# Update of the sample states in a decoder layer: 32-row products against block-masked rows, replaced by 12-row products in four row tiles, with the state index on partitions

## The chip, the cores and the metric

One core of one Trainium2 chip. The metric is the device time of one launch in microseconds (us). The engines of the core are PE (TensorE, matmuls), DVE (VectorE), ACT (ScalarE), POOL (GpSimd) and SP (SyncE). In this kernel SP issues most loads and POOL issues most stores; neither computes anything to speak of.

## The reference

One layer of a hybrid decoder with d_model 2048. 288 token columns go through it: 256 of one prompt and 8 sample sequences of 4 tokens each. Cut to what matters here:

```python
proj = rmsnorm(x) @ w_in                 # s_in, z, xbc, dt, two gates
ya   = sgu_branch(s_in)                  # u * (W_s LN(v) + b)
yb, h_new = mamba_branch(z, xbc, dt, conv_buf, h0)
x = x + (sigmoid(ga) * (ya @ w_out_a) + sigmoid(gb) * (yb @ w_out_b)) @ w_o
x = x + (silu(h2 @ w_gate) * (h2 @ w_up)) @ w_down         # h2 = rmsnorm(x)

# the state of one sample sequence after its four tokens; 64 heads of
# 64 channels p, 128 state numbers n, 8 heads share one group's b_in
h_new[p, n] = exp(cs[last]) * h0[p, n]
            + sum_l  exp(cs[last] - cs[l]) * dt[l] * x[l, p] * b_in[l, n]
```

The change concerns the last line for the sample sequences: 8 sequences x 64 heads x 64 x 128 numbers, 16.8 MB read and as much written. The sum runs over the four tokens of one sequence only. The numbers are fp32 throughout. A product in full precision is made of three quick ones: each operand is split into a high part (rounded to the type fp32r) and a low part, and high x high, high x low and low x high are added.

## The kernel before, in words

**The weight units.** Nearly all of PE's stream is products of weights with 288 token columns: records `pm<-hh,wh` and the like, 128x128 weights against 128x288. The weights come from HBM in pieces of 512 KB (`raw`, four buffers, loaded by SP), ACT casts a piece to `wh`, DVE subtracts to make `wl`, three buffers each. The list `ORDER` sets the sequence of units: input projection (channels u, v, z, x, b, c, gates), the products with w_out_a and w_out_b (`A`, `B`; the rows `yb` are the right sides of w_b), then w_o and the feed-forward part.

**The planner.** Everything else is written as Python generators (`g_ssd`, `g_gate`, `g_upd` and others), and a planner, the class `Plan`, lays them between the weight products when the program is built. It keeps a clock for each engine from rough costs. After each k-step of a unit `side()` asks every open generator, in order of its priority, whether what it waits for (`yield x`: data; `yield "name"`: a milestone) is ready by these clocks, and if so lets it write its next instructions. Before a unit's products `need()` runs the generators until the right side has been written. On the chip every engine then runs its own list strictly in that order, and waits by semaphores where data isn't there. A `yield` in a generator is therefore a place where weight products may be put.

**Buffers.** Tiles come from pools with fixed numbers of buffers: q (25, of 4x288 columns), t (7, of 630 columns), x (4 PSUM banks of 512 columns), m (2 PSUM pairs for the units). `K.res("t")` waits until the planner has one free, `K.rel("t")` and `K.drop()` (for q) give them back. How many a generator asks for thus moves it, and others, in the order.

**Groups.** The state-space part has 8 groups g of 8 heads. `g_ssd(g)` transposes and scales the group's rows; it stores the 32 sample tokens' b rows (`bt`, to `scr_bs`) and their weighted x rows (`xw`, to `scr_xs`) to scratch memory in HBM, and sets the milestone `fin{g}`. `g_gate(g)` makes the gated and normalised rows yb of group g (its norm is the product `rms`), split into `ybh` and `ybl`. `g_upd(g)`, with the lowest priority, starts after the unit marker "late" (behind the gate units `gb`), after `fin{g}` and after `g_upd(g - 1)`.

**The update.** `g_upd(g)` loads `scr_xs` and `scr_bs` three times over into 96 partitions, by six loads on SP's queue: the row blocks 0, 32 and 64 hold high, high and low parts of x against high, low and high parts of b, so that one product of 96 rows has the three terms. `bk` is b laid out eight times, multiplied with a mask (`C_BM`) that keeps the rows of sequence b only. For each pair of heads j of the group there are a load of 512 KB of states `su`, 128 channels on the partitions and 8 sequences x 128 state numbers in the columns, two products `up` of 512 columns, eight instructions `K.stt` that multiply 128x128 of the state with its decay (`etot`, one number for each partition and sequence) and add the product, and a store on POOL's queue. `K.load` uses SP's queue unless told otherwise, `K.store` POOL's.

Of the kernel before, what the change touches and what calls it, by code (L numbers as in the profile page):

```python
# [6 lines left out]
F32 = mybir.dt.float32  # L7
F32R = mybir.dt.float32r
I32 = mybir.dt.int32
AF = mybir.ActivationFunctionType  # L10
ALU = mybir.AluOpType

T, P, S, NB, L = 288, 256, 32, 8, 4
# [2 lines left out]
EPS = 1e-6  # L16


C_ID, C_TRI, C_ONE, C_SUF, C_MB, C_MBS, C_PAR, C_JM, C_BM, C_SEL, C_NEG, C_MP, C_JB = (
    0, 128, 256, 512, 640, 672, 704, 832, 864, 872, 904, 1032, 1160)  # L20
C_W = 1288
V_G1, V_G2, V_GF, V_NG, V_DS, V_CW, V_CB, V_DT, V_AL = 0, 16, 32, 48, 80, 112, 304, 352, 353
V_W = 354

# [383 lines left out]
def trunk(ctx, tc, io):  # L408
    ND = 6
    K = Plan(ctx, tc, io)  # L410
    nc = tc.nc
# [232 lines left out]
    wds = K.const([128, 16], "wds")  # L644
    csm = K.const([128, 8, 2, S], "csm")
    ecs = K.const([128, 64], "ecs")
    etot = K.const([128, 32, NB], "etot")

    def g_dt(ps):
        qa = yield from K.q([4, T], "dta")  # L650
# [70 lines left out]
        for j in range(4):  # L721
            for i in range(2):
# [8 lines left out]
        K.act(et, csr[:, P:T].rearrange("p (b l) -> p b l", l=L)[:, :, 3], AF.Exp)  # L731
        yield et
        K.rel("x", 2)
        em = K.tmp([64, 32, NB], "em")
        K.mul(em, et.unsqueeze(1).to_broadcast([64, 32, NB]),
              cst[0:64, C_JM:C_JM + 32].unsqueeze(2).to_broadcast([64, 32, NB]))
        yield em
        yield from K.res("x")
        pe = K.ps("etot")
        K.mm(pe[:, 0:256], cst[0:64, C_PAR:C_PAR + 128], em.rearrange("p j b -> p (j b)"), True, True)  # L740
        yield pe
        K.copy(etot, pe[:, 0:256].rearrange("p (j b) -> p j b", j=32))
        K.rel("x")
        K.rel("t")
        K.drop(2)
# [108 lines left out]
    def g_ssd(g):  # L854
# [33 lines left out]
        bt = K.tmp([128, 4, 128], "bt")  # L888
        K.copy(bt[:, 0:2], p1[:, 0:P].rearrange("p (c n) -> p c n", c=2))
        K.copy(bt[0:32, 2], p1[0:32, P:384])  # L890
        K.store(io["scr_bs"][g], bt[0:32, 2])
        for c in range(2):
            p1 = K.ps("xt")
            for j in range(4):
# [20 lines left out]
                    K.mm(pf[:, j * 128:j * 128 + 128], xd[:, c, j * 128:j * 128 + 128], bt[:, c], c == 0, c == 1)  # L915
        xw = K.tmp([128, 128], "xw")
        K.mul(pair(xw), pair(xts), wide(wds[:, H2]))
        K.store(io["scr_xs"][g], xw)
        K.sub(ms, csm[:, g], css[:, H2].unsqueeze(2).to_broadcast([128, 2, S]))
        K.ts(ms, ms, 0.0, ALU.min)  # L920
        yield ms
# [101 lines left out]

    def g_upd(g):
        yield ["late", f"fin{g}", f"upd{g - 1}"]
        yield from K.res("q", 2)
        yield from K.res("t", 2)
        xf, b3 = K.tmp([96, 512], "xf"), K.tmp([96, 3, 128], "b3")
        for r in range(3):
            K.load(xf[32 * r:32 * r + 32].rearrange("t (j c) -> t j c", j=4), io["scr_xs"][g].rearrange("(j t) c -> t j c", j=4))  # L1030
            K.load(b3[32 * r:32 * r + 32, 0], io["scr_bs"][g])
        sk = K.q_now([2, 512], f"sk{g}", F32R)[0:96]
        bh = sk[:, 1, 0:128]
        yield [xf, b3]
        K.copy(sk[:, 0], xf)
        K.copy(bh, b3[:, 0])
        yield sk
        K.sub(sk[64:96, 0], xf[64:96], sk[64:96, 0].bitcast(F32))
        K.vcopy(b3[:, 1], bh.bitcast(F32))
        K.sub(b3[32:64, 1], b3[32:64, 0], bh[32:64].bitcast(F32))  # L1040
        sk = sk[:, 0]
        bk = K.q_now([NB, 128], f"bk{g}", F32R)[0:96]
        K.mul(bk, b3[:, 1].unsqueeze(1).to_broadcast([96, NB, 128]),
              cst[0:96, C_BM:C_BM + NB].unsqueeze(2).to_broadcast([96, NB, 128]))
        K.rel("t", 2)
        yield None
        for j in range(4):
            st = yield from K.q([NB, 128], f"su{g}{j}")
            K.load(st, io["st_p"][4 * g + j])
            yield st  # L1050
            yield from K.res("x", 2)
            pu = [K.ps(f"up{i}") for i in range(2)]
            bf = bk.rearrange("p b n -> p (b n)")
            for i in range(2):
                K.mm(pu[i], sk[:, 128 * j:128 * j + 128], bf[:, 512 * i:512 * i + 512], True, True, f32=False)
            yield [st] + pu
            for b in range(NB):
                K.stt(st[:, b], st[:, b], etot[:, 4 * g + j, b:b + 1], pu[b // 4][:, 128 * (b % 4):128 * (b % 4) + 128],
                      ALU.mult, ALU.add)
                if b == 3:  # L1060
                    yield None
            K.rel("x", 2)
            yield st
            K.store(io["new_ssm_s"][4 * g + j], st)
            K.drop()
        K.drop(2)
        K.have.add(f"upd{g}")

    K.have.add("upd-1")
# [303 lines left out]
def _constants():  # L1373
    import numpy as np

    c = np.zeros((128, C_W), np.float32)
    i = np.arange(128)
    c[:, C_ID:C_ID + 128] = np.eye(128)
    c[:, C_TRI:C_TRI + 128] = i[:, None] <= i[None, :]
    c[:, C_ONE:C_ONE + 128] = 1  # L1380
    c[:, C_ONE + 128:C_ONE + 256] = c[:, C_TRI:C_TRI + 128]
    c[:, C_NEG:C_NEG + 128] = np.where(i[:, None] <= i[None, :], 0, -1e30)
    c[:, C_SUF:C_SUF + 128] = i[:, None] > i[None, :]
    s = i[:32]
    blk = s[:, None] // 4 == s[None, :] // 4
    c[:32, C_MB:C_MB + 32] = blk & (s[:, None] <= s[None, :])
    c[:32, C_MBS:C_MBS + 32] = blk & (s[:, None] > s[None, :])

    at = 32 * (s % 16 // 4) + 4 * (s // 16) + s % 4
    c[:32, C_MP + at] = c[:32, C_MB:C_MB + 32]  # L1390
    c[at, C_SEL + s] = 1
    for j in range(4):
        c[32 * j:32 * j + 32, C_JB + 32 * j:C_JB + 32 * j + 32] = blk & (s[:, None] <= s[None, :])
    h = i[:64]
    c[:64, C_PAR:C_PAR + 128] = h[:, None] % 2 == i[None, :] // 64
    c[:64, C_JM:C_JM + 32] = h[:, None] // 2 == s[None, :]
    c[:96, C_BM:C_BM + 8] = (i[:96, None] % 32) // 4 == i[None, :8]
    return c


def _layout(f):
    import numpy as np

    f = {k: np.asarray(v) for k, v in f.items()}
    ca = np.ascontiguousarray
    lay = lambda w: ca(w.reshape(w.shape[0] // 128, 128, w.shape[1] // 256, 256).transpose(2, 1, 0, 3))
    chan = lambda v: v.reshape(-1, 128).T
    x = np.concatenate([f["x_prompt"].reshape(P, D), f["x_sample"].reshape(S, D)], 0)
    w = f["w_in"][0]
    wt = w.reshape(16, 128, w.shape[1])  # L1410
    dev = {}
    dev["x"] = ca(x.T.reshape(16, 128, T).transpose(1, 0, 2))
    vec = np.zeros((128, V_W), np.float32)
    vec[:, V_G1:V_G1 + 16] = chan(f["norm1_g"][0])
    vec[:, V_G2:V_G2 + 16] = chan(f["norm2_g"][0])
    vec[:, V_GF:V_GF + 16] = chan(f["final_norm_g"])
    vec[:, V_NG:V_NG + 32] = chan(f["ssm_norm_g"][0])
    vec[:, V_DS:V_DS + 32] = chan(np.repeat(f["d_skip"][0], 64))
    vec[:, V_CW:V_CW + 192] = f["conv_w"][0].reshape(4, 48, 128).transpose(2, 1, 0).reshape(128, 192)
    vec[:, V_CB:V_CB + 48] = chan(f["conv_b"][0])  # L1420
    vec[64:, V_DT] = f["dt_bias"][0]
    vec[:64, V_AL] = f["a_log"][0]
    dev["vec"] = vec
    dev["cst"] = _constants()
    dev["stc"] = ca(f["state_conv"][0].reshape(24, 48, 128).transpose(2, 1, 0))
    sw = f["sgu_w"][0]
    dev["swt"] = ca(sw.transpose(2, 0, 1))
    swb = np.zeros((128, 16, 32), np.float32)
    for b in range(8):
        swb[4 * b:4 * b + 4, :, 4 * b:4 * b + 4] = sw[:, :4, :4].transpose(2, 0, 1)  # L1430
    dev["swb"] = swb
    dev["sgb"] = ca(f["sgu_b"][0])
    dev["lng"] = ca(f["sgu_ln_g"][0])
    dev["lnb"] = ca(f["sgu_ln_b"][0])
    cols = _win_columns()
    wi = np.empty((len(cols), 128, 16, 256), np.float32)
    for n, c in enumerate(cols):
        wi[n] = wt[:, :, c:c + 256].transpose(1, 0, 2)
    dev["w_in"] = wi
    dev["w_dt"] = ca(wt[:, :, 14336:14400].transpose(1, 0, 2))  # L1440
    dev["w_a"] = lay(f["w_out_a"][0])
    dev["w_b"] = np.stack([lay(f["w_out_b"][0][2048 * i:2048 * i + 2048]) for i in range(2)])
    dev["w_o"] = lay(f["w_o"][0])
    g = f["w_ffn_gate"][0].reshape(16, 128, JT, 128)
    u = f["w_ffn_up"][0].reshape(16, 128, JT, 128)
    dev["w_gu"] = ca(np.stack([g, u], 3).transpose(2, 1, 0, 3, 4).reshape(JT, 128, 16, 256))
    dev["w_d"] = np.stack([lay(f["w_ffn_down"][0][2816 * i:2816 * i + 2816]) for i in range(2)])
    st = f["state_ssm"][0].reshape(8, 8, 512, 128)
    dev["st_n"] = ca(st.transpose(1, 3, 0, 2).reshape(8, 128, 4096))
    dev["st_p"] = ca(f["state_ssm"][0].reshape(8, 32, 128, 128).transpose(1, 2, 0, 3))  # L1450
    return dev


_OUT = {
    "y": (128, 16, T), "new_ssm_p": (8, 128, 512), "new_conv": (128, 48, 27), "new_ssm_s": (32, 128, 8, 128), "new_v": (32, 2048),
}
_SCR = {"scr_cs": (64, T), "scr_a": (8, 128, 2, T), "scr_b": (8, 128, 2, T),
        "scr_xs": (8, 128, 128), "scr_bs": (8, 32, 128),
        "scr_xd": (8, 128, 2, 512), "scr_bt": (8, 128, 2, 128)}


# [30 lines left out]
```

## Time and profile before

| | before |
|---|---|
| median of 3 runs | 2320.87 us (2320.67 to 2321.26) |
| profiled execution, its own time | 2320.45 us |
| its span in the trace | 2318.7 us |
| mean granted TensorE clock | 0.998 |
| PE busy | 2304.2 us, 99% |
| DVE busy | 1431.4 us, 62% |
| ACT busy | 1001.0 us, 43% |
| POOL busy | 88.7 us, 4% |
| HBM read, written | 421.65 MB, 31.54 MB |

How such a profile is read. Times are in us from the start of the span. A group's row has line, engine, operation, output<-inputs by the program's names, sizes, and `x` count; after the first bar the busy time in all and the mean length in ns of one, after the second the idle time of the engine just before them and what ended it. A row of waits has the instruction that waited, `<-` what it waited for, then the sum in us, the count and the longest. A row of the timeline has start and length, engine, line, the instruction; `x16` means that sixteen stand together, and a bracket holds idle time ahead of it. A row of DMA issues has the count, then minimum/median/maximum of the issue in ns, and below the time from issue to landing. A row by windows has the stretch A:B, its length, and for PE, PEld (weight load), DVE, ACT and POOL the busy time with the number of instructions; then the granted clock, the DMA engines' busy share and GB/s. Matmuls are pipelined: one lasts about 0.3 us and the next starts 0.13 us after it.

### The profile page before, as it was taken

How to read it: one execution, taken by the hardware profiler on the slowest of the kernel's cores; microseconds unless marked ns; L12 is line 12 of the kernel's file. 1: busy time of each engine (PE TensorE's matmuls, PEld its weight loads, DVE VectorE, ACT ScalarE, POOL GpSimd, SP SyncE). 2: the span in 40 equal slices, each digit the busy share in tenths (PEclk: the TensorE clock that was granted, in tenths of full speed). 3: DMA queues.
4: the chain of work that ended last, by engine and by line, in shares of the span. 5: the costliest groups of instructions: out<-in, count | busy, mean ns of one | idle time of the engine just before them, and what ended most of it. 6: DMA issues, size and time to landing. Idle time of an engine off the chain costs nothing.

```text
span 2318.7 us, 42525 instructions
## 1 busy us (share of the span) xinstructions
PE 2304.2 (99%) x17571; PEld 2271.5 (98%) x17571; DVE 1431.4 (62%) x2216; ACT 1001.0 (43%) x1425; POOL 88.7 (4%) x187
## 2 busy tenths in 40 slices
PE   9999999999999989999999999999999999999999
PEld 8999999999999989999999999999999999999999
DVE  7687553446887875477865767766664444545444
ACT  6453433335654645455433334433333333333333
POOL 0000000001110000010000000000000000000000
PEclk9999999999999999999999999999999999999999
DMA  8465686666667556565567877676775555555654
GB/s 290 132 210 149 199 285 190 180 185 193 188 188 229 152 168 190 174 189 150 176 216 246 284 239 250 216 222 218 227 227 167 167 170 165 168 165 164 229 168 140
DMA packets 151106, 455.96 MB, mean 197 GB/s; under 512 B 20848, under 2 KB 40560, under 8 KB 150912
## 3 DMA queue, kind: packets, MB, share of 16 engines
q1 hardware_dynamic: 140528, 424.06, 59.5%
q0 software_dynamic: 9376, 27.62, 3.3%
q8 instruction: 137, 2.24, 0.4%
q10 hardware_dynamic: 1008, 1.58, 0.2%
q14 instruction: 57, 0.47, 0.1%
HBM read 421.65 MB, written 31.54 MB: 195 GB/s over the span
## 4 chain that ended last, share of the span: by engine, by line
PE 99%; DVE 1%; DMA 0%; ACT 0%; issue 0%; SPq 0%; ACTq 0%; DVEq 0%
PE pm L187 94%; PE y L187 1%; PE up L187 1%; PE fin L187 1%; PE yoff L187 1%; PE mix L187 0%; PE xt L193 0%; PE cb L187 0%; DMA x<-x 0%; DVE wl L152 0%; PE va L193 0%; PE rms L187 0%; PE btok L193 0%; DVE xs L170 0%; DVE acc L170 0%
## 5 line engine op out<-in xcount | busy, mean ns | idle before, releaser
L152 DVE TENSOR_TENSOR wl<-raw,wh 128x1024 fp32r<-128x1024 f32 (+2 forms) x700 | 835.1, 1193 | 830.3 <-ACT wh L183 822.8
L183 ACT CAST wh<-raw 128x1024 fp32r<-128x1024 f32 (+2 forms) x704 | 717.6, 1020 | 1094.6 <-PE pm L187 796.3
L187 PE MATMUL pm<-hh,wh 128*128 128x288 f32 x2128 | 632.5, 297 | 0.0
L187 PE MATMUL pm<-hl,wh 128*128 128x288 f32 x2128 | 627.6, 295 | 0.0
L187 PE MATMUL pm<-hh,wl 128*128 128x288 f32 x2112 | 623.8, 295 | 0.0
L187 PE MATMUL pm<-xgl,wh 128*128 128x288 f32 x1408 | 415.8, 295 | 0.0
L187 PE MATMUL pm<-xgh,wl 128*128 128x288 f32 x1408 | 415.8, 295 | 0.0
L187 PE MATMUL pm<-xgh,wh 128*128 128x288 f32 x1408 | 414.5, 294 | 0.6 <-DVE ff L152 0.6
L187 PEld LDWEIGHTS pm<-hh,wh 128*128 128x128 f32 x2128 | 400.1, 188 | 9.5 <-issue 8.1
L187 PEld LDWEIGHTS pm<-hl,wh 128*128 128x128 f32 x2128 | 399.7, 188 | 0.2
L187 PEld LDWEIGHTS pm<-hh,wl 128*128 128x128 f32 x2112 | 396.7, 188 | 0.2 <-DVE wl L152 0.2
L187 PEld LDWEIGHTS pm<-xgh,wh 128*128 128x128 f32 x1408 | 264.2, 188 | 1.5 <-issue 0.8
L187 PEld LDWEIGHTS pm<-xgl,wh 128*128 128x128 f32 x1408 | 264.7, 188 | 0.7
L187 PEld LDWEIGHTS pm<-xgh,wl 128*128 128x128 f32 x1408 | 264.4, 188 | 0.0
L187 PE MATMUL pm<-fl,wh 128*128 128x288 f32 x704 | 207.9, 295 | 0.0
L187 PE MATMUL pm<-fh,wl 128*128 128x288 f32 x704 | 207.8, 295 | 0.0
L187 PE MATMUL pm<-fh,wh 128*128 128x288 f32 x704 | 207.2, 294 | 0.0
L187 PE MATMUL pm<-ybh,wh 128*128 128x288 f32 x512 | 153.2, 299 | 6.1 <-ACT ybh L183 6.1
L187 PE MATMUL pm<-ybl,wh 128*128 128x288 f32 x512 | 152.5, 298 | 0.8 <-DVE ybl L152 0.8
L187 PE MATMUL pm<-ybh,wl 128*128 128x288 f32 x512 | 152.4, 298 | 0.0
L187 PEld LDWEIGHTS pm<-fl,wh 128*128 128x128 f32 x704 | 132.3, 188 | 0.0
L187 PEld LDWEIGHTS pm<-fh,wl 128*128 128x128 f32 x704 | 132.2, 188 | 0.0
(254 smaller groups left out, 2809.8 us busy)
## 6 DMA issues: line engine op xcount, KB each, us to landing
raw<-w_in SPq DMA_DIRECT2D x284, 512.0 KB, 4.0
raw<-w_gu SPq DMA_DIRECT2D x176, 512.0 KB, 3.9
raw<-w_d SPq DMA_DIRECT2D x75, 512.0 KB, 3.6
raw<-w_b SPq DMA_DIRECT2D x64, 512.0 KB, 4.4
st<-st_n SPq DMA_DIRECT2D x32, 512.0 KB, 6.3
raw<-w_a SPq DMA_DIRECT2D x32, 512.0 KB, 3.9
su<-st_p SPq DMA_DIRECT2D x32, 512.0 KB, 5.7
new_ssm_s<-su POOLq DMA_DIRECT2D x32, 512.0 KB, 3.4
```

The lines of the kernel that those rows point to most:

```text
L152: self.nc.vector.tensor_tensor(out, a, b, op=op)
L183: self.nc.scalar.copy(out, a)
L187: self.nc.tensor.matmul(out, lhsT, rhs, start=start, stop=stop)
```

## The change

`g_upd` is written anew. The state index n is on the 128 partitions now, and the columns are 8 sequences x 512 channels, the layout that the input `st_n` already has; the input `st_p` goes, and the output `new_ssm_s` changes its layout. A sequence has 4 tokens, so its three terms need 12 rows. Four sequences stand at the partitions 0, 32, 64 and 96, with 12 rows each, and their four products (weights `bk` 12x128, right side `xk` 12x512) go to the array's four row tiles, into four PSUM banks: all of pool x. A group takes two such halves h. The decay `etot` is now the same on all partitions and lies along the columns; DVE multiplies the state with it before the products (two instructions of 1024 columns for a half), and adds the products afterwards (four of 512).

The rows `xk` and `bk` are gathered by 36 loads for each group, on POOL's queue. The splitting in high and low parts moves from `g_upd` to `g_ssd`, which asks for one more t buffer (`xb`) for that, and stores both parts. In `g_dt` the product for `etot` has 512 columns where it had 256.

```diff
@@ g_dt
-        em = K.tmp([64, 32, NB], "em")
-        K.mul(em, et.unsqueeze(1).to_broadcast([64, 32, NB]),
-              cst[0:64, C_JM:C_JM + 32].unsqueeze(2).to_broadcast([64, 32, NB]))
+        em = K.tmp([64, NB, 64], "em")
+        K.mul(em, et.unsqueeze(2).to_broadcast([64, NB, 64]),
+              cst[0:64, C_ID:C_ID + 64].unsqueeze(1).to_broadcast([64, NB, 64]))
...
-        K.mm(pe[:, 0:256], cst[0:64, C_PAR:C_PAR + 128], em.rearrange("p j b -> p (j b)"), True, True)
+        K.mm(pe, K.one[0:64], em.rearrange("p b h -> p (b h)"), True, True)
...
@@ g_ssd
-        K.store(io["scr_bs"][g], bt[0:32, 2])
...
-        K.store(io["scr_xs"][g], xw)
+        yield from K.res("t")
+
+        xb = K.tmp([128, 4, 128], "xb", F32R)
+        K.hilo(xb[0:32, 2], xb[0:32, 3], bt[0:32, 2])
+        K.store(io["scr_bs"][g].rearrange("a t n -> t a n"), xb[0:32, 2:4])
+        yield xw
+        K.hilo(xb[:, 0], xb[:, 1], xw)
+        K.store(io["scr_xs"][g].rearrange("a p c -> p a c"), xb[:, 0:2])
+        K.rel("t")
...
@@ g_upd (the lines before stand above)
+        yield from K.res("q")
+        yield from K.res("t")
+
+        xk, bk = K.q_now([2, 512], f"xk{g}", F32R), K.tmp([128, 2, 128], "bk", F32R)
+        for r in range(4):
+            for i, (a, b) in enumerate(((0, 0), (0, 1), (1, 0))):
+                o = slice(32 * r + 4 * i, 32 * r + 4 * i + 4)
+                for h in range(2):
+                    K.load(xk[o, h].rearrange("l (j c) -> l j c", j=4),
+                           io["scr_xs"][g, a].rearrange("(j h r l) c -> h r l j c", j=4, h=2, r=4)[h, r], nc.gpsimd)
+                K.load(bk[o], io["scr_bs"][g, b].rearrange("(h r l) n -> r l h n", h=2, r=4)[r], nc.gpsimd)
+        yield [xk, bk]
+        for h in range(2):
+            yield from K.res("q", 2)
+            st = [K.q_now([2, 512], f"su{g}{h}{i}") for i in range(2)]
+            for i, t in enumerate(st):
+                K.load(t, io["st_n"][g, :, 2048 * h + 1024 * i:2048 * h + 1024 * i + 1024].rearrange("p (b c) -> p b c", b=2))
+            for i, t in enumerate(st):
+                yield t
+                v = t.rearrange("p b (h d) -> p b h d", h=8)
+                e = etot[:, 4 * h + 2 * i:4 * h + 2 * i + 2, 8 * g:8 * g + 8]
+                K.mul(v, v, e.unsqueeze(3).to_broadcast([128, 2, 8, 64]))
+            yield from K.res("x", 4)
+            pu = [K.ps(f"up{r}") for r in range(4)]
+            for r in range(4):
+                o = slice(32 * r, 32 * r + 12)
+                K.mm(pu[r], bk[o, h], xk[o, h], True, True, f32=False)
+            yield st + pu
+            for i, t in enumerate(st):
+                for k in range(2):
+                    K.add(t[:, k], pu[2 * i + k], t[:, k])
+                K.rel("x", 2)
+                K.store(io["new_ssm_s"][g, :, 2048 * h + 1024 * i:2048 * h + 1024 * i + 1024].rearrange("p (b c) -> p b c", b=2), t)
+                yield None
+            K.drop(2)
+        K.drop()
+        K.rel("t")
         K.have.add(f"upd{g}")
```

What the planner makes of it is not in the diff. The numbers behind names in the following listings count tiles, `DMASW` and `DMAHW` are the semaphores of the DMA lanes (POOL's queue uses eight lanes, DMASW0 to 7, in turn), and a bracket holds what a row waits for.

POOL's queue around the end of one group's update, before: the stores of the states, one for each pair of heads, and each waits for DVE's last instruction on its tile.

```order
L202 DMA new_ssm_s<-su_12988 128x1024 [waits DMAHW3_49,DMASW2_49,DVE_49]
L202 DMA new_ssm_s<-su_13200 128x1024 [waits DMAHW2_49,DMASW3_49,DVE_49]
L202 DMA new_ssm_s<-su_13370 128x1024 [waits DMAHW0_49,DMASW4_49,DVE_49]
L202 DMA new_ssm_s<-su_13646 128x1024 [waits DMAHW7_49,DMASW5_49,DVE_49]
L202 DMA new_ssm_s<-su_13783 128x1024 [waits DMAHW4_49,DMASW6_49,DVE_49]
```

After: the last two stores of a group, and behind them the first of the next group's 36 loads.

```order
L201 DMA new_ssm_s<-su_13037 128x1024 [waits DMAHW5_49,DMASW7_49,DVE_49]
L201 DMA new_ssm_s<-su_13038 128x1024 [waits DMAHW6_49,DMASW0_49,DVE_49]
L196 DMA xk_13230<-scr_xs 4x4x128 [waits DMAHW1_49,DMASW1_49,Activation_49]
L196 DMA xk_13230<-scr_xs 4x4x128 [waits DMASW2_49]
L196 DMA bk<-scr_bs 4x2x128 [waits DMASW3_49]
L196 DMA xk_13230<-scr_xs 4x4x128 [waits DMASW4_49]
L196 DMA xk_13230<-scr_xs 4x4x128 [waits DMASW5_49]
```

The loads stand between the stores of one group and those of the next, and each waits for the landing of the transfer that used its lane before, the eighth ahead of it.

PE's list at one update's products, before (`hh` and `hl` are the high and low parts of the normalised rows):

```order
L187 MATMUL pm<-hh_943,wl 128x288
L187 MATMUL up_13714<-bk_13631,sk_13545 128x512
L187 MATMUL up_13715<-bk_13631,sk_13545 128x512
L187 MATMUL pm<-hh_943,wh 128x288
L187 MATMUL pm<-hl_944,wh 128x288
```

After, at the first half of a group:

```order
L186 MATMUL pm<-hh_943,wl 128x288
L186 MATMUL up_13426<-xk_13230,bk 128x512 [waits DMASW6_49,DMASW4_49,DMASW7_49,DMASW3_49,DMASW1_49]
L186 MATMUL up_13427<-xk_13230,bk 128x512 [waits DMASW5_49,DMASW4_49,DMASW7_49,DMASW2_49,DMASW0_49]
L186 MATMUL up_13428<-xk_13230,bk 128x512 [waits DMASW5_49,DMASW3_49,DMASW6_49,DMASW1_49,DMASW0_49]
L186 MATMUL up_13429<-xk_13230,bk 128x512 [waits DMASW6_49,DMASW4_49,DMASW7_49,DMASW2_49,DMASW1_49]
L186 MATMUL pm<-hh_1051,wh 128x288 [waits Activation_49]
```

Pairs have become fours, and the products wait for the lanes of POOL's loads; the weight products of the unit stand behind them.

PE's list also moved at the first unit of w_b, where the rows of groups 3 and 4 are prepared. Before, ahead of the first of the yb products (62 rows ahead of it) stood the norm's product of gate group 3, then the first products of `g_ssd(4)`:

```order
L187 MATMUL pm<-hh_785,wl 128x288
L187 MATMUL rms<-rmp,oner 128x288 x2
L187 MATMUL cb<-c_3315,bf 128x256
L187 MATMUL cb<-c_3315,bf 128x128
L187 MATMUL cb<-c_3315,sm 128x32
L187 MATMUL pm<-hh_785,wh 128x288
```

After, the same two things stand behind the first 72 yb products:

```order
L186 MATMUL pm<-ybl_8808,wh 128x288
L186 MATMUL pm<-ybh_8617,wl 128x288
L186 MATMUL cb<-c_3315,bf 128x256
L186 MATMUL cb<-c_3315,bf 128x128
L186 MATMUL cb<-c_3315,sm 128x32
L192 MATMUL btok<-cst,bf 128x128 x2
L192 MATMUL btok<-cst,bf 32x128
L192 MATMUL xt<-cst,xs_8802 128x128 x8
L192 MATMUL xts<-cst,sm 128x128
L186 MATMUL rms<-rmp,oner 128x288 x2
L186 MATMUL pm<-ybh_9470,wh 128x288
```

Of the second listing, the products of group 4's preparation (`cb`, `btok`, `xt`, `xts`) and the norm of gate group 3 have come to stand between the yb products of group 2 and those of group 3.

More of the change, by code (lines that the diff above doesn't have):

```diff
@@ L16 @@
 EPS = 1e-6
-C_ID, C_TRI, C_ONE, C_SUF, C_MB, C_MBS, C_PAR, C_JM, C_BM, C_SEL, C_NEG, C_MP, C_JB = (
-    0, 128, 256, 512, 640, 672, 704, 832, 864, 872, 904, 1032, 1160)
-C_W = 1288
+C_ID, C_TRI, C_ONE, C_SUF, C_MB, C_MBS, C_SEL, C_NEG, C_MP, C_JB = 0, 128, 256, 512, 640, 672, 704, 736, 864, 992
+C_W = 1120
 V_G1, V_G2, V_GF, V_NG, V_DS, V_CW, V_CB, V_DT, V_AL = 0, 16, 32, 48, 80, 112, 304, 352, 353
@@ L646, in trunk @@
     ecs = K.const([128, 64], "ecs")
-    etot = K.const([128, 32, NB], "etot")
+    etot = K.const([128, NB, 64], "etot")
     def g_dt(ps):
@@ L739, in g_dt @@
         pe = K.ps("etot")
-        K.mm(pe[:, 0:256], cst[0:64, C_PAR:C_PAR + 128], em.rearrange("p j b -> p (j b)"), True, True)
+        K.mm(pe, K.one[0:64], em.rearrange("p b h -> p (b h)"), True, True)
         yield pe
-        K.copy(etot, pe[:, 0:256].rearrange("p (j b) -> p j b", j=32))
+        K.copy(etot, pe.rearrange("p (b h) -> p b h", b=NB))
         K.rel("x")
@@ L1025, in g_upd @@
         yield ["late", f"fin{g}", f"upd{g - 1}"]
[L1026 to L1065, printed above, removed]
@@ L1066, in g_upd @@
-        K.drop(2)
+        yield from K.res("q")
[8 more added lines that the diff above has]
+                K.load(bk[o], io["scr_bs"][g, b].rearrange("(h r l) n -> r l h n", h=2, r=4)[r], nc.gpsimd)
@@ L1393, in _constants @@
         c[32 * j:32 * j + 32, C_JB + 32 * j:C_JB + 32 * j + 32] = blk & (s[:, None] <= s[None, :])
[L1394 to L1397, printed above, removed]
     return c
@@ L1449, in _layout @@
     dev["st_n"] = ca(st.transpose(1, 3, 0, 2).reshape(8, 128, 4096))
-    dev["st_p"] = ca(f["state_ssm"][0].reshape(8, 32, 128, 128).transpose(1, 2, 0, 3))
     return dev
 _OUT = {
-    "y": (128, 16, T), "new_ssm_p": (8, 128, 512), "new_conv": (128, 48, 27), "new_ssm_s": (32, 128, 8, 128), "new_v": (32, 2048),
+    "y": (128, 16, T), "new_ssm_p": (8, 128, 512), "new_conv": (128, 48, 27), "new_ssm_s": (8, 128, 4096), "new_v": (32, 2048),
 }
 _SCR = {"scr_cs": (64, T), "scr_a": (8, 128, 2, T), "scr_b": (8, 128, 2, T),
-        "scr_xs": (8, 128, 128), "scr_bs": (8, 32, 128),
+        "scr_xs": (8, 2, 128, 128), "scr_bs": (8, 2, 32, 128),
         "scr_xd": (8, 128, 2, 512), "scr_bt": (8, 128, 2, 128)}
@@ L1472 @@
     for n, s in _SCR.items():
-        io[n] = nc.dram_tensor(n, s, F32, kind="Internal").ap()
+        io[n] = nc.dram_tensor(n, s, F32R if n in ("scr_xs", "scr_bs") else F32, kind="Internal").ap()
     with tile.TileContext(nc) as tc, ExitStack() as ctx:
@@ L1479 @@
     sp = o["new_ssm_p"].reshape(8, 128, 4, 128).transpose(0, 2, 1, 3)
-    ss = o["new_ssm_s"].transpose(2, 0, 1, 3)
+    ss = o["new_ssm_s"].reshape(8, 128, NB, 512).transpose(2, 0, 3, 1)
     cv = o["new_conv"].transpose(2, 1, 0).reshape(27, 6144)
```

## The prediction

> **What bounds the kernel now.** I read the page first: engines, clock row, chain.
>
> ```profile
> PE 2304.2 (99%) x17571; PEld 2271.5 (98%) x17571; DVE 1431.4 (62%) x2216; ACT 1001.0 (43%) x1425; POOL 88.7 (4%) x187
> PEclk9999999999999999999999999999999999999999
> PE 99%; DVE 1%; DMA 0%; ACT 0%; issue 0%; SPq 0%; ACTq 0%; DVEq 0%
> ```
>
> TensorE has work from end to end. A change is worth what it takes out of PE's stream, less every microsecond for which PE has to wait. So I next read PE's waits, and the stretch around the longest one by windows.
>
> ```profile
> PE pm L187 <- ACT ybh L183: 6.1, 1, 6.1
> PE pm L187 <- DVE ybl L152: 0.8, 1, 0.8
> ...
> 834.00:841.00 7.00, 7.00 (x55) 7.00 (x54) 5.21 (x14) 3.19 (x4) 1.44 (x3) 1.00 0.53 153
> 841.30:847.40 6.10, 0.00 (x0) 0.00 (x0) 6.00 (x13) 1.61 (x2) 0.67 (x2) 0.76 0.90 283
> 847.40:854.70 7.30, 6.49 (x25) 6.18 (x26) 4.26 (x11) 1.44 (x3) 0.29 (x1) 0.50 0.22 80
> 855.00:862.00 7.00, 7.00 (x55) 7.00 (x54) 4.13 (x6) 6.75 (x16) 0.54 (x1) 1.00 0.41 121
> ```
>
> There is one long wait, 6.1 us, at the first unit of w_b, for the gated rows yb. DVE is busy for 6.00 of it with 13 instructions (0.46 us each). A wait costs more than itself: after it the granted clock is 0.50 for 7.3 us and 25 matmuls pass. At the normal pitch (0.133 us, next fence) they take 3.3, and 0.8 is the second wait, so 3.2 us were lost behind a wait of 6.1.
>
> **The products themselves.** PE's own time for `up`, from the timeline:
>
> ```profile
> 1161.52 0.62 PE L187 MATMUL up<-bk,sk 96*128 96x512 f32 x2
> 1161.97 0.30 PE L187 MATMUL pm<-hh,wh 128*128 128x288 f32 x1
> 1162.11 0.29 PE L187 MATMUL pm<-hl,wh 128*128 128x288 f32 x1
> 1162.23 0.30 PE L187 MATMUL pm<-hh,wl 128*128 128x288 f32 x1
> ```
>
> A pair holds the array from 1161.52 to 1161.97, 0.45 us, 0.225 for each product of 512 columns; 32 pairs are 14.4 us. After the change there are again 64 products of 512 columns, in 16 groups of four. What four cost is open: this trace has no row tiles. The nearest rows are column tiles, the yoff products:
>
> ```profile
> 288.29 0.30 PE L187 MATMUL pm<-hh,wl 128*128 128x288 f32 x1
> 288.51 1.93 PE L187 MATMUL yoff<-st,cm 128*32 128x512 f32 x16
> 290.37 0.40 PE L187 MATMUL pm<-hh,wh 128*128 128x288 f32 x1
> 290.61 0.30 PE L187 MATMUL pm<-hl,wh 128*128 128x288 f32 x1
> ...
> L187 PE MATMUL yoff<-st,cm 128*32 128x512 f32 x128 | 15.4, 598 | 0.0
> ```
>
> 128 records of 598 ns are 76.5 us of work in 15.4 us of busy time: tiles overlap. The switch has a price: 0.22 instead of 0.13 us before the first tile, 0.24 instead of 0.13 behind, and about 0.1 to empty, 0.3 us for both ways. By these rows a group takes 0.225 + 0.3 = 0.53 us, 16 groups 8.4, a gain of 6.0 us. The ends: without any switch price 3.6 us, a gain of 10.8; without overlap 4 x 0.225 + 0.3 = 1.2 us, 19.2 in all, a loss of 4.8. I take the gain of 6.0, by the nearest row.
>
> The Trainium skill's page "TensorE: Matmul & The Clock Gate" (Part 3, measured speedup) gives four row tiles of 512 columns as 3.07 times faster than one after the other. By it a group would take 0.30 us without a switch, and the sum would end 3.5 us lower; no run here shows it.
>
> ```profile
> L187 PE MATMUL etot<-em,cst x2: 376/428/480, 155.9 to 156.2; 64*128 64x256 f32 x2
> ```
>
> The etot product doubles to 512 columns; its two records now stand 0.3 us apart, so +0.6 us, in PE's stream at 156 us.
>
> **What feeds the products.** This is the term that decides. The loads of xk and bk go to POOL's queue, 36 for each g, where six went to SP's. In the program the 36 of group g+1 stand right behind the last store of group g (the listing above). That store waits for DVE's last add of g, and PE's four products of g+1 wait for the loads' lanes; behind them PE has all the weight matmuls queued. So the whole chain from add to products has to fit between two products in PE's stream. Its parts:
>
> ```profile
> L202 POOL DMA_DIRECT2D scr_bs<-bt x8: 511/511/513, 562.3 to 1044.0; - x8
> DMA to landing us min/median/max: 1.7/3.2/4.2
> ...
> L202 POOL DMA_DIRECT2D new_conv<-ncv x48: 537/538/695, 136.0 to 1022.7; - x48
> DMA to landing us min/median/max: 1.7/3.4/5.5
> ...
> 610.22 0.54 POOL L202 DMA_DIRECT2D scr_xd<-xd  x1 [4.35 <-DVE xts L152]
> 610.75 0.54 POOL L202 DMA_DIRECT2D scr_bt<-bt  x1
> ...
> 1062.23 0.54 POOL L202 DMA_DIRECT2D new_ssm_p<-fin  x1 [4.17 <-ACT fin L183]
> ...
> 1162.71 2.15 DVE L170 SCALAR_TENSOR_TENSOR su<-su,etot,up 128x128 f32<-128x128 f32 x8
> 1165.16 0.54 POOL L202 DMA_DIRECT2D new_ssm_s<-su  x1 [102.39 <-DVE su L170]
> ...
> L183 ACT CAST wh<-raw 128x1024 fp32r<-128x1024 f32 x663 | 694.4, 1048 | 1043.5 <-PE pm L187 749.8 <-issue 259.3 <-DMA raw<-w_gu 6.4
> L152 DVE TENSOR_TENSOR wl<-raw,wh 128x1024 fp32r<-128x1024 f32 x663 | 811.2, 1224 | 795.7 <-ACT wh L183 788.3 <-DMA b<-scr_bs 4.0 <-PE pm L187 1.9
> L152 DVE TENSOR_TENSOR xt<-xt,dtk 128x512 f32<-128x512 f32 x16 | 10.9, 683 | 1.2 <-PE xt L193 1.2
> ```
>
> POOL takes 0.51 to 0.54 us for an issue, whatever its size, and two in a row start 0.53 apart. So: 0.3 us from DVE's end (1164.86) to the store (1165.16), 0.5 for the store, 36 x 0.54 = 19.4 for the loads, 3.4 until the last one lands: 23.6 us from the last add.
>
> The room: from the second half's products of g to the first half's of g+1, PE's listing has 157, 145, 157, 211, 163, 193 and 193 matmuls for the seven successions, 174 on average, 23.2 us at 0.133. The adds use up part of it: on DVE they stand behind the next wl, which needs a cast (1.05) and a split (1.22) after PE has freed a buffer, and four adds of at most 0.68 follow; by the matmuls that stand between the products and the adds in the program, the last add ends 5 to 10 us behind the products, 7.1 on average. 16.1 us are left for 23.6. PE waits 7.5 us, seven times: +53 us. The first group pays nothing: POOL's last earlier row is a store at 1062 us.
>
> The bounds of this: issue at 0.51 and landing in 1.7 make 20.9, a wait of 4.8, +34. If landing takes 5.5, it also holds back the issue: each load waits for the lane of the eighth before it, 5.5 / 8 = 0.69 us each, 24.8 + 5.5 + 0.8 = 31.1, a wait of 15, +105.
>
> The page "DMA: Bandwidth & Descriptors" of the Trainium skill (Anatomy of one DMA, SWDGE path) puts about 2.0 us on a small transfer. By it the chain is 22.2 us, the wait 6.1, and the sum 10 us lower; the medians here, 3.2 and 3.4, are longer and decide.
>
> Each wait is long enough for the halved clock seen above: 3.2 us lost behind a wait of 6.1. That price holds a second wait which kept the clock down; I take 2.5, with 0 and 3.2 as ends: 7 x 2.5 = +17 (0 to 22).
>
> **The wait for yb.** g_ssd now asks for one more t buffer, so the planner places the steps of groups 3 and 4 otherwise. Before, the rms product of group 3 stood 62 rows ahead of the first yb matmul; now it stands 72 matmuls behind it, and the whole gate chain of group 3 and half the preparation of group 4 lie between. From the y evacuation, which now stands right ahead of the yb matmuls, to the first ybl DVE has 52 instructions; at 0.46 us that is 24 us. 9.6 are covered by the 72 matmuls, and PE's own products in between take about 2.4:
>
> ```profile
> 821.95 0.43 PE L187 MATMUL rms<-rmp,oner 128*128 128x288 f32 x2
> 822.21 0.81 PE L187 MATMUL cb<-c,bf 128*128 128x256 f32 x4
> ...
> 829.79 0.60 PE L193 MATMUL xt<-cst,xs 128*128 128x128 f32 x4
> 831.01 0.60 PE L193 MATMUL xt<-cst,xs 128*128 128x128 f32 x4
> ```
>
> (xt twice.) 12 us remain against 6.9 before: +5. The ends are 0, if the reordering lets DVE start earlier, and +10, since three of the 52 are wl at 1.22.
>
> **Costed at nothing.**
>
> ```profile
> L170 DVE SCALAR_TENSOR_TENSOR su<-su,etot,up 128x128 f32<-128x128 f32 x256 | 69.8, 341 | 0.1
> L152 DVE TENSOR_TENSOR bk<-b,cst 96x1024 fp32r<-96x1024 f32 x8 | 9.8, 1221 | 0.3
> L152 DVE TENSOR_TENSOR sk<-xf,sk 32x512 fp32r<-32x512 f32 x8 | 5.5, 683 | 0.3
> ```
>
> DVE loses work for each g: 32 multiply-adds of 0.34 (10.9 us), bk 1.2 and sk 0.7, 12.8 in all. In their place stand 4 multiplications of 1024 columns (as wl, 1.22) and 8 adds of 512 (as xt, 0.68), 10.4. PE is the bound, so this gives nothing. If DVE fell behind, the adds would come later and the waits would grow. SP issues 48 small loads fewer; nothing waited for them.
>
> **Sum.** The profiled execution took 2320.45 us (span 2318.7 and 1.75 around it), 0.4 below the median of 2320.87. 2320.45 - 6.0 + 0.6 + 53 + 17 + 5 = 2390.
>
> **Rivals.** Hidden loads: if POOL's chain fits, only 2320.45 - 6.0 + 0.6 + 0 to 5 is left, 2315 to 2320. The place is the 36 issues; it decides below (16.1 - 4.2) / 36 = 0.33 us for one. Against it: no POOL issue in this trace is under 0.51. Chance 0.05.
>
> Short waits: 4.8 us each, the clock mostly kept, 2320.45 - 6 + 0.6 + 5 + 34 = 2354, or lower if the adds come at the 5 us end of their range: 2340. For it: the least landings. Chance 0.12.
>
> Lane-bound loads: landing 5.5 us under the load traffic, 2320.45 - 6 + 0.6 + 5 + 105 + 22 = 2447; half way is 2430. For it: the longest landings of new_conv; against it: the medians. Chance 0.11.
>
> Row tiles that do not overlap: +10.8 us on any of these, inside their widths.
>
> My forecast, waits of 5 to 12 us before seven of the eight groups, has 0.72, at 2350 to 2430; leaving out a little of both neighbours, 2346 to 2432 holds 8 in 10. 0.2% (4.6 us) is about what can be told from no change. Slower: all but the hidden case, 0.95; the hidden case is split, 0.02 faster and 0.03 the same.
>
> **What would show it.** Seven entries among PE's waits, up on a DMA of xk or bk, of about 7 us; the halved clock behind them; POOL with 36 issues in a row, 0.54 apart, up to the end of each wait; four up matmuls of the second half starting within some ns of each other if the tiles overlap; the wait for ybh near 12 us. Wrong it is if POOL issues faster than 0.51, or if the loads are found to start ahead of the last store.

## The result, and the profile after

The changed kernel takes 2434.70 us (median of 4 runs, 2429.76 to 2435.41), the kernel before 2320.90: ratio 1.0485, 95% interval 1.0469 to 1.0502. It was forecast as slower, and by waits for the loads of xk and bk, but at 2390 with an upper end of 2432. The loss is 114 us instead of 69. The direction came out, and so did the wait for these loads as its main cause; the size did not, because the 36 loads take longer than the sum had them.

The page after: engines, clock row, chain.

```profile
PE 2332.1 (96%) x17571; PEld 2284.4 (94%) x17571; DVE 1426.1 (59%) x2040; ACT 999.1 (41%) x1425; POOL 255.1 (10%) x475
PEclk9999999999999989999978988999999999999999
PE 84%; DMA 6%; issue 5%; POOL 3%; DVE 1%; ACT 1%; SPq 0%; POOLq 0%; ACTq 0%; DVEq 0%
```

PE no longer has work from end to end, and the clock row has dents between slices 22 and 29, where the updates are. The waits of PE:

```profile
PE up L186 <- DMA bk<-scr_bs: 55.8, 14, 6.7
PE up L186 <- DMA xk<-scr_xs: 20.6, 4, 6.1
PE pm L186 <- ACT ybh L182: 8.3, 1, 8.3
...
PE rms L186 <- ACT rmp L182: 1.6, 1, 1.6
...
PE rms L186 <- DVE rmp L151: 1.5, 1, 1.5
PE pm L186 <- DVE ybl L151: 1.1, 1, 1.1
```

Besides the wait for ybh, which the kernel before has too, `up` waits on xk and bk in 18 pieces, 76.4 us. Two stretches of PE's timeline show a group whose loads were early (the first) and one whose loads were late (the second):

```profile
1169.40 0.29 PE L186 MATMUL pm<-hh,wl 128*128 128x288 f32 x1
1169.62 0.51 PE L186 MATMUL up<-xk,bk 12*128 12x512 f32 x4
1170.06 0.40 PE L186 MATMUL pm<-hh,wh 128*128 128x288 f32 x1
1170.30 0.29 PE L186 MATMUL pm<-hl,wh 128*128 128x288 f32 x1
...
1208.90 0.29 PE L186 MATMUL pm<-hh,wl 128*128 128x288 f32 x1
1209.12 0.50 PE L186 MATMUL up<-xk,bk 12*128 12x512 f32 x1
1215.63 0.76 PE L186 MATMUL up<-xk,bk 12*128 12x512 f32 x1 [6.02 <-DMA bk<-scr_bs]
1219.06 0.76 PE L186 MATMUL up<-xk,bk 12*128 12x512 f32 x1 [2.66 <-DMA bk<-scr_bs]
1223.83 0.76 PE L186 MATMUL up<-xk,bk 12*128 12x512 f32 x1 [4.01 <-DMA bk<-scr_bs]
1224.52 0.61 PE L186 MATMUL pm<-hh,wh 128*128 128x288 f32 x1
1224.92 0.44 PE L186 MATMUL pm<-hl,wh 128*128 128x288 f32 x1
1225.16 0.44 PE L186 MATMUL pm<-hh,wl 128*128 128x288 f32 x1
```

Undisturbed, all four products stand within 0.51 us from the first start to the last end: the row tiles overlap. Late, the four start one by one: the first when PE comes to it, the other three each 0.1 to 0.2 us after the last of their own nine loads has landed. The last starts 14.7 us after the first, and the weight products behind it start 0.24 us apart instead of 0.13. POOL in that succession, and the windows of the halved clock:

```profile
1193.82 0.53 POOL L201 DMA_DIRECT2D new_ssm_s<-su  x1 [18.67 <-DVE su L151]
1195.02 0.53 POOL L201 DMA_DIRECT2D new_ssm_s<-su  x1 [0.66 <-DVE su L151]
1195.63 0.60 POOL L196 DMA_DIRECT2D xk<-scr_xs  x1
...
1221.72 0.56 POOL L196 DMA_DIRECT2D bk<-scr_bs  x1
```

```profile
L196 POOL DMA_DIRECT2D xk<-scr_xs x24 | 13.7, 574 | 5.5 <-DMA xk<-scr_xs 3.5 <-DMA new_ssm_s<-su 1.8
L196 POOL DMA_DIRECT2D bk<-scr_bs x12 | 6.8, 564 | 0.9 <-DMA xk<-scr_xs 0.6 <-issue 0.4
...
DMA to landing us min/median/max: 1.9/4.6/8.0
```

```profile
1274.10:1280.00 5.90, 5.90 (x25) 5.72 (x25) 0.69 (x1) 0.00 (x0) 0.56 (x1) 0.50 0.29 117
```

The store waits for the last add, the 36 loads follow, from 1195.63 to 1222.28: 26.65 us, of which 20.5 are POOL's own and the rest waits, for the landing of earlier loads and of the stores in the same lanes. In the last window the granted clock is 0.50.

The seven late successions, from the starts and ends in the trace, mean us beside what the prediction had:

| piece | predicted | measured |
|---|---|---|
| second half's products of g to first half's of g+1 | 23.2 | 23.62 |
| products to the end of the last add | 7.1 | 7.29 |
| last add to the first load's issue | 0.8 | 0.88 |
| the 36 issues, first start to last end | 19.4 | 26.90 (25.5 to 28.6) |
| last issue's end to the last product | 3.4 | 1.54 |
| first product to last product of the group | 7.5 | 12.99 (10.1 to 15.8) |

How long a load takes to land goes with the traffic around it. Two windows of the third late succession, the first with PE still at work and the second with PE waiting for the loads:

```profile
1299.30:1313.60 14.30, 14.30 (x109) 14.17 (x107) 8.69 (x10) 5.61 (x6) 9.46 (x17) 1.00 1.03 371
1318.50:1327.90 9.40, 1.41 (x2) 0.42 (x2) 0.00 (x0) 0.00 (x0) 7.02 (x13) 0.50 0.09 10
```

At 371 GB/s the first loads of this succession land after 5 to 8 us; at 10 GB/s the last ones land after 2. While PE waits, ACT and DVE have no weight piece to split (0 instructions in the second window), and the traffic falls away. Over all 288 loads, the 96 that took over 5.5 us to land had 321 GB/s around them on average, the 58 that took under 2.2 us had 16.

### The profile page after: what moved, and what is told of

Read it like the earlier page. It is cut to its first block, busy times and chain, and to the rows that moved or that the text cites. A ratio compares the mean times of both kernels' runs of the same rounds, so it can differ in the third digit from the quotient of the medians.

```text
span 2433.5 us, 42674 instructions
## 1 busy us (share of the span) xinstructions
PE 2332.1 (96%) x17571; PEld 2284.4 (94%) x17571; DVE 1426.1 (59%) x2040; ACT 999.1 (41%) x1425; POOL 255.1 (10%) x475
## 4 chain that ended last, share of the span: by engine, by line
PE 84%; DMA 6%; issue 5%; POOL 3%; DVE 1%; ACT 1%; SPq 0%; POOLq 0%; ACTq 0%; DVEq 0%
PE pm L186 80%; DMA xk<-scr_xs 3%; POOL xk L196 2%; PE y L186 1%; DMA new_ssm_s<-su 1%; DMA su<-st_n 1%; DMA bk<-scr_bs 1%; POOL bk L196 1%; PE fin L186 1%; PE yoff L186 1%; PE mix L186 0%; DVE wl L151 0%; ACT wh L182 0%; POOL new_ssm_s L201 0%; PE xt L192 0%
```

## The experiments

The theory: the loss is PE waiting for the chain store, 36 issues, landing, with a halved clock behind each wait, and on top of it an order at yb that has nothing to do with row tiles. The rivals: the loads cost by their number or traffic wherever they stand; the row tiles themselves are dear.

**Fewer loads, same place.**

```diff
-                for h in range(2):
-                    K.load(xk[o, h] ..., io["scr_xs"][g, a] ... [h, r], nc.gpsimd)
+                K.load(xk[o], io["scr_xs"][g, a].rearrange("(h r l) c -> r l h c", h=2, r=4)[r], nc.gpsimd)
```

(For this layout the rows of x are stored in two stores instead of one.)

> 24 loads for a group instead of 36 (scratch laid out so that one load holds both halves), at the same place on POOL's queue. Chain theory: after the change the 36 issues took 26.3 us on average, 0.73 each with the lane waits; 24 take 17.5, so PE's wait ahead of a group falls from 12.9 to about 4 us, seven times, with perhaps 3 us of halved clock each: 2320.5 - 6 + 6 (yb) + 28 + 21 = 2370, between 2350 and 2385. Rival, cost lies in the switch to row tiles or in the new instructions of PE and DVE: the time stays within 10 us of 2434. Rival, cost goes with the number of loads whatever they hold up (extra traffic, small packets): a third of the loss goes, 2397.

2390.96 us, ratio 1.0301 (1.0286 to 1.0317).

```profile
PE up L186 <- DMA bk<-scr_bs: 29.7, 12, 4.1
...
PE up L186 <- DMA xk<-scr_xs: 3.8, 1, 3.8
```

Over the range of the chain theory, but far from the first rival's 2434. The 24 issues took 18.6 us (17.5 expected, 0.78 each), 13.7 of it POOL's own time, the last landing 3.2 behind them, where it was 1.5 with 36; the wait from first to last product fell from 13.0 to 6.3, not to 4. The halved clock behind a wait cost 2.15 us each, though the waits were half as long. This run alone doesn't decide against a cost by number (2397).

**Eight loads.** Scratch memory holds, for each row tile, its three parts side by side.

```diff
+        for r in range(4):
+            o = slice(32 * r, 32 * r + 12)
+            K.load(xk[o], io["scr_xs"][g, :, r].rearrange("h i l c -> (i l) h c"), nc.gpsimd)
+            K.load(bk[o], io["scr_bs"][g, :, r].rearrange("h i l n -> (i l) h n"), nc.gpsimd)
...
-        K.store(io["scr_xs"][g].rearrange("a p c -> p a c"), xb[:, 0:2])
+        for i, a in enumerate((0, 0, 1)):
+            for j in range(4):
+                K.store(io["scr_xs"][g, :, :, i, :, 128 * j:128 * j + 128].rearrange("h r l c -> (h r) l c"), xb[32 * j:32 * j + 32, a])
```

(scr_bs in the same way, three stores.)

> 8 loads for a group (scratch memory holds the three parts for each row tile side by side; 15 stores ahead of them in the group's preparation, where there were 2). Chain theory: 8 issues of 0.57 and a landing of 4 us make 9.4 us from the last add, against 16 us of room: no waits of up, 2320.5 - 6.4 (up) + 0.6 + 6 (yb) = 2321, between 2316 and 2326. Rival, cost with the number of loads: two ninths of the loss stay, about 2345. Rival, stores on POOL's queue take the part of the loads: 2 us each in the preparation, above 2330.

2326.82 us, ratio 1.0029 (1.0017 to 1.0041). The waits of PE:

```profile
PE pm L186 <- ACT ybh L182: 8.3, 1, 8.3
...
PE pm L186 <- DVE xgl L151: 1.0, 1, 1.0
PE up L186 <- DVE nt L165: 0.7, 1, 0.7
```

No wait for a load is left; 108 of the 114 us are gone, though the time ends 0.8 above the range forecast.

**36 loads, a group earlier.**

```diff
+    def g_ld(g):
+        yield ["late", f"fin{g}", f"ld{g - 1}", f"upd{g - 2}"]
...                                   (the buffers and the 36 loads of g_upd)
+        kb[g] = xk, bk
+        K.have.add(f"ld{g}")
```

> The same 36 loads on the same queue, but those of group g+1 are issued a group earlier, behind the last store of g-1 (a generator of its own, one more buffer of each pool). Chain theory: their 26 us lie beside a whole group's time and up waits for none of them: 2321, between 2316 and 2332 (the states' stores stand behind 36 loads on POOL now and give their buffers back later, which may cost some us). Rival, the loads themselves cost (traffic, lanes): they are all still there, so the time stays above 2400.

2326.75 us, ratio 1.0028 (1.0016 to 1.0040). The number of loads is the same, and POOL took even longer for the 36 (32.0 us), but no product waits for them. The time is that of the version with 8 loads, so the loads have no price by themselves; their place has. This excludes the rival by number. The 6 us that are left over the kernel before are those of the order at yb (below).

**36 loads on SP.** The same loads with `nc.sync`, their rows declared as plain fp32 for the transfer.

> The same 36 loads at the same place of the program, on SP's queue, which doesn't hold the stores. Chain theory: they no longer wait for the last add, so PE's waits for xk and bk go; but SP needs about 0.42 us for such an issue (as for xf before), 15 us for 36, in which no weight piece is asked for, while PE uses one in 3.2 us and four buffers are ahead: waits for wl of about 5 us a group instead, 2320.5 - 6 + 6 + 8 x 5 + clock 15 = 2375, between 2330 and 2400. Rival, the queue doesn't matter, only the number of loads: 2434 within 10.

2363.81 us, ratio 1.0192 (1.0175 to 1.0209).

```profile
PE pm L186 <- ACT wh L182: 9.5, 5, 3.5
...
PE pm L186 <- DVE wl L151: 4.3, 6, 0.9
PE pm L186 <- DVE lb L151: 3.6, 1, 3.6
PE pm L186 <- DVE x L151: 2.4, 1, 2.4
```

As the theory said, `up` waits no more for xk and bk, and PE waits for weights (wh, wl) and reloaded rows (lb, x) instead, whose loads stand behind the 36 on SP. It was less than expected: an issue took SP 0.30 us at the median, not 0.42.

**The order at yb, alone in the kernel before.**

```diff
         K.store(io["scr_xs"][g], xw)
+        yield from K.res("t")
+        yield xw
+        K.rel("t")
```

> The kernel before with one thing of the change alone: the preparation of a group asks for one more t buffer and has one more yield at the place where the change splits x and b (no instruction is added). Its list for PE has the norm of gate group 3 behind the first 72 yb products, as after the change. Theory: this order costs what the kernel with 8 loads had lost ahead of its first up product, 8 us: 2327 to 2328. Rival, the splitting itself (ACT and DVE instructions, stores) makes the yb wait longer: no change, 2320.

2326.95 us, ratio 1.0028 (1.0017 to 1.0039): 6.3 us for three lines that compute nothing.

```profile
PE pm L187 <- ACT ybh L183: 7.6, 1, 7.6
PE rms L187 <- ACT rmp L183: 1.7, 1, 1.7
...
PE rms L187 <- DVE rmp L152: 1.5, 1, 1.5
PE pm L187 <- DVE ybl L152: 1.1, 1, 1.1
```

The wait at the first yb product is 1.8 us longer (8.7 with ybl, 6.9 before); new are the two waits of `rms`, 3.2 us, which now stands among the yb products, and the halved clock goes on longer (13.7 us in the record of the granted clock, 10.2 before).

**Eight loads with the order of before, or with the splitting elsewhere.** The split parts go to unused columns of `xw` and `bt`, so no more buffer is asked for.

```diff
-        yield from K.res("t")
-        xb = K.tmp([128, 4, 128], "xb", F32R)
-        K.hilo(xb[0:32, 2], xb[0:32, 3], bt[0:32, 2])
+        was = dict(K.clk), dict(K.rdy)
+        xb, bb = xw[:, 1:3].bitcast(F32R), bt[0:32, 2:4].bitcast(F32R)
+        K.hilo(bb[:, 1], bb[:, 0], bt[0:32, 2])
...
-        yield xw
...
+        K.clk.update(was[0])
+        K.rdy.update(was[1])
```

> 8 loads for a group, and the split parts kept in unused columns of buffers that the preparation holds anyway, with no yield there and the planner's clocks put back behind it, so that the order at the yb products is that of before. Theory: the 8 us go, and the 5 to 6 us that the row tiles save are left: 2326.8 - 8 = 2319, between 2315 and 2321, at or just under before. Rival, the splitting itself is what makes the wait: 2327.

2320.46 us, ratio 1.0000 (0.9991 to 1.0009): the 6 us of the order are back, the saving of 5 is not to be seen. In the other version the block stands behind the exponential instead, and the planner counts it:

> As the one with the order of before at yb, but the splitting stands behind the exponential of the preparation and the planner counts it: the norm of gate group 3 then stands 85 rows ahead of the first yb product instead of 62. If each row ahead is worth 0.13 us of the wait, the wait falls from 6.9 to about 4 us and some of the halved clock behind it goes: 2316, between 2311 and 2322. Rival, the wait is set by DVE's work and not by this distance: as the other, 2319.

2318.87 us, ratio 0.9994 (0.9985 to 1.0003). Its waits for yb:

```profile
PE pm L186 <- DVE ybl L151: 2.4, 1, 2.4
...
PE pm L186 <- ACT ybh L182: 1.5, 1, 1.5
```

The wait fell to 3.9, as expected; the time fell by 1.6 us, less than the two medians can settle.

**The same edit in the changed kernel with 36 loads.**

> The change with its 36 loads, but the split parts in buffers that are held anyway, so that the order at the yb products is that of before (the same edit as in the kernel with 8 loads and that order). If the waits for the loads and the order at yb are separate costs, the time falls by the 6 to 8 us that the order cost elsewhere: 2427 to 2429. Rival, the two hang together (the order moves the groups' spacing): another change, by 15 us or more.

2426.48 us, ratio 1.0457 (1.0442 to 1.0471): 8.2 less than the change (7.5 when each is set against the kernel before in its own series of runs), the waits for loads unchanged at 76.0 us. The two costs add up.

**The four products apart.** In the version with 8 loads and the order of before, a `yield None` between the four.

> As the kernel with 8 loads and the order of before at yb, but between the four products of a half stand 6 weight products each (a yield between them), so that row tiles can't run beside one another. Theory, overlap is where the saving comes from: each product pays 0.225 us and the switch in and out, 0.53 us, 64 of them 33.9 instead of 8.4: 25 us more, 2344. Rival, 12 rows are quick by themselves, whatever stands beside them: below 2325.

2348.09 us, ratio 1.0117 (1.0103 to 1.0130): 27.6 more.

```profile
1165.23 0.29 PE L186 MATMUL pm<-hh,wl 128*128 128x288 f32 x1
1165.45 0.50 PE L186 MATMUL up<-xk,bk 12*128 12x512 f32 x1
1165.88 0.40 PE L186 MATMUL pm<-hh,wh 128*128 128x288 f32 x1
1166.12 0.29 PE L186 MATMUL pm<-hl,wh 128*128 128x288 f32 x1
```

One product alone takes the same stretch as four: 1165.23 to 1166.12 is 0.89 us here, 1169.40 to 1170.30 is 0.90 in the first timeline of the change. By all records, one costs PE 0.62 us over the normal pitch and four cost 0.634. The three more are nearly free, which excludes the rival. Of the 0.62, 0.23 is what one product of a pair takes in the kernel before; the other 0.39 stand at its two borders, where PE goes into the row tiles and out again.

**Eight loads, early, with either order.** Both edits from above together.

> The version with 8 loads whose splitting stands behind the exponential, with the loads also issued a group earlier, which spaces the updates closer and takes the last one away from the norm at the end of w_o, where the kernels with 8 loads wait 1.2 us (up for a PSUM buffer) and 1.3 us (the first right sides of the feed-forward). If these two waits go: 2318.9 - 2.5 = 2316.5, between 2314 and 2320, 0.1 to 0.2% under before. Rival: the waits move elsewhere, 2319.

2316.84 us, ratio 0.9988 (0.9979 to 0.9997): 0.1% under the kernel before, with an interval that ends just under 1. Its waits no longer have the one of `up` for a PSUM buffer:

```profile
PE pm L186 <- DVE ybl L151: 2.4, 1, 2.4
PE rms L186 <- DVE rmp L151: 1.6, 1, 1.6
...
PE pm L186 <- ACT ybh L182: 1.5, 1, 1.5
PE pm L186 <- DVE mgl L169: 1.0, 1, 1.0
```

> The same with the order of before at the yb products: 2320.5 - 2.5 = 2318, between 2315.5 and 2321. Rival: the waits move elsewhere, 2320.5.

2318.37 us, ratio 0.9994 (0.9985 to 1.0003). In both versions, of the two waits the one of `up` has gone; in the place of the 1.0 for xgl there is 1.0 for mgl.

## Why the prediction was wrong in size

**The products.** Right in kind: the same 64 products, tiles that overlap. I had taken 0.45 us for a pair and 0.53 for four, a saving of 6.0. Over the normal pitch a pair costs 0.467 (32 pairs). Four cost 0.53 up to the next weight product and 0.106 more on the one behind it: 10.1 against 14.9, a saving of 4.8. The Trainium skill ("TensorE: Matmul & The Clock Gate", Part 3, measured speedup) has four row tiles of 32 rows at 3.07 times. By 4 x 0.62 against 0.634 it is 3.9 here with 12 rows, where each lone product pays the switch as well. (By the prediction's own terms the 3.07 would have moved the sum by 16 x (0.53 - 0.30) = 3.7 us, not 3.5.)

**What feeds them.** This is the step that failed: "36 x 0.54 = 19.4 for the loads". It had the waits for lanes at nothing, and it measured 26.9. 1.2 us are POOL's own time (0.57 for such a gather instead of 0.54, 20.6 in all), the other 6.3 are waits between the issues, 5.5 of them for the landing of an earlier transfer by the trace. The mechanism stood in the prediction, but only in its upper bound and in the rival "Lane-bound loads": a lane comes round every 8 x 0.57 = 4.6 us, and the median landing of the xk loads is 4.6 us with a maximum of 8.0, so about half of the loads land later than their lane is wanted again. I had set the lane against the medians 3.2 and 3.4 of small stores, which stand in a quieter stretch: 186 GB/s from 560 to 1044 us of the trace before, 241 from 1195 to 1565, where the updates run. The other pieces of the chain up to the loads were right to 0.5 us.

The last landing was shorter than taken, 1.54 us behind the issues instead of 3.4, and hid 1.9 of the 7.5 us by which the issues were too low. The Trainium skill's page "DMA: Bandwidth & Descriptors" (Anatomy of one DMA, SWDGE path) has about 2.0 us for a small transfer. From the start of its issue the last load landed after 1.9 us, which agrees; the loads ahead of it, with medians of 4.6 (xk) and 4.3 us (bk), are far above that figure. From the first product to the next weight product, less what four undisturbed ones take, the seven waits are 92.7 us where 53 stood. (The 76.4 in the list of waits leave out PE's time in the lone products.)

The rival "Lane-bound loads", 2447 with a chance of 0.11, is the nearest to what happened, in its mechanism too. Its wait of 15 us was near the 13.0 measured because two errors met: 24.8 for the issues was too low, 5.5 for the last landing too high. Its "half way is 2430" is a slip: half way between 2390 and 2447 is 2419.

**The halved clock.** Some 130 weight products behind the seven waits stand 0.24 us apart, the first of each 0.41, instead of 0.133: 14.7 us, 1.3 to 2.8 each; 17 stood in the sum.

**The wait for yb.** +5 stood in the sum. 6.3 (alone in the kernel before) to 8.2 (taken out of the change) were measured. The wait came out as four instead of one: 8.3 + 1.1 + 1.6 + 1.5 = 12.5. That is near the 12 predicted, but by luck: the wait that was worked out, for the first yb, is 9.4 of it, and the two of `rms` were not foreseen. Left out was that the halved clock lasts longer, 17.1 us by the record of the granted clock where it was 10.2. One point of the argument was wrong: the t buffer is not needed for the shift. With the buffer gone and the `yield xw` left, PE's listing has the norm of group 3 at the same place behind the 72 yb products; no run was made of that.

**The sum.** -4.8 + 0.6 + 92.7 + 14.7 + 8 = 111, against 115 between the two profiled executions. 1.2 more are the wait of the last half's products for a PSUM buffer that the norm at the end of w_o holds (`nt`), 1.3 the wait for the feed-forward's first rows; what is left is some 2 us by which this execution was late at its 1100th weight product. 0.6 of that is etot; 1.6 were there at the 100th already, where the executions of the other versions are 0.1 to 1.9 late. In the versions without the load waits these small ones are as large as the saving, which is why it doesn't show in the times until they go too. Counted from the 7900th weight product, just ahead of the updates, to the end, the traces show it: against the kernel before, the version with 8 loads and the order of before gains 2.4 us, and the one with its loads early as well 4.2 of the 4.8.

What stays open: how much of a long landing is due to weight loads and how much to state loads. The landings go with the traffic around them, and where PE doesn't wait (36 loads a group earlier) the last twelve of a group land after 4.5 us on average instead of 2.7; but no run took the traffic away and left the rest as it was.

## What to carry to other kernels

Where an operand is gathered by many small transfers on an in-order queue, write the time from what releases the queue to the last landing, and price each transfer at the larger of its issue and the landing divided by the lanes, with the landing under load. Even that was too low here: with each load's own landing it gives 24.1 us for the 36, with the median landing 20.7, and 26.9 were measured. If the chain doesn't fit, change the place first: the same 36 loads a group earlier cost no more than eight loads. When a generator gains a `yield` or a buffer, look at the order far from the change: three lines that compute nothing cost 6 us.

## What I had not expected of the hardware

A halved clock cost about 2 us, and the length of the wait ahead of it hardly mattered: 1.3 to 2.8 behind waits of 10 to 16 us, and 1.6 to 2.6 behind the 3 to 9 us of the version with 24 loads. And three further row tiles were nearly free: 0.634 us for four products of 12 rows and 512 columns, 0.62 for one.
